# A hybrid attention, S5 and convolution layer on one core: the first head's loads in another order, the S5 branch's tables in another order and further apart, its Toeplitz loads on another queue

## The chip, the core and the metric

The kernel runs on one core of one Trainium2 chip. A core has a matrix engine (TensorE, PE in the profile, with its weight loads as PEld), VectorE (DVE), ScalarE (ACT), GpSimd (POOL), and SyncE (SP), which here only issues transfers. Every engine takes its instructions in the order in which they stand in its queue. The metric is the time of one launch in device microseconds (us); less is better.

## What is computed

One layer of a streaming encoder trunk, for a prompt of 2048 frames of one new stream and for 64 new frames of a running stream with 2048 cached frames. The width is 1024. The normed input is projected; eight attention heads of 64 with a forget gate, an S5 state-space branch and a gated short convolution each make a part of `mix`; an out-projection and a feed-forward layer of 4096 follow.

```python
h = _rms(x, lp['ln1']); proj = h @ lp['w_in']          # q, k, v, forget gate, u, conv inputs
s = q k^T * HEAD_DIM**-0.5 + c_q - c_k                  # c: cumulative log forget gate
p = softmax(where(k_pos <= q_pos, s, NEG_INF)); att = p @ v
h_t = a * h_(t-1) + bbar u_t ;  y = Re(c h) + d u       # S5: 16 groups of 16 channels, 64 complex states
ssm = g * sigmoid(g @ w_glu + b_glu),  g = gelu(y)
conv = gate_b * sum_j w[j] z[t + j],   z = gate_c * hc
x = x + concat[_rms(att), _rms(ssm), _rms(conv)] @ w_out
x = x + relu(_rms(x) @ w_up)**2 @ w_down
```

## The kernel before

The work runs in phases: the in-projection with the first head's row maxima (`phase1`), attention (`attention`), the out-projection, the up- and the down-projection. The change touches only the attention phase, and the loads that stand ahead of it.

**Heads.** A head is 24 units of one or two key tiles of 128 against 512 queries. A unit (`scores`) makes scores `st` in two matmuls (L1239 from `kb` and `q1`, L1240 from `ka` and `q2`), their exponential `p` and its rounded part `ph` on ACT (L1248, L1251), the rest `pl` on DVE (L1252), and, two and three units later, the sums `po` with `v3` (L1260, L1262, L1267). Beside them stand the row maxima of the next head: `mx` on PE (L1149, L1153) and `pm` on DVE (L1154). `load(h)` brings a head's `kb`, `q1` and `ka`; `load_q2` brings one quarter of the queries as `q`, `load_v` the values. `load(h + 1)` is issued at the start of head h. All are issued by SP, in its order. Of the first head, `load(0)` also issues its first `q` and its `v`, and ACT issues a small transfer of its row maxima (`m_d<-mt`, then `q<-m_d`).

**The background.** After each unit `fill(w)` draws steps from a generator, `chain()`: the S5 branch, the attention of the 64 sample frames, and the preparation of the out-projection. A step that yields n is followed only when a clock has moved on by n; the clock moves by 1.68 times the unit's cost, so a bigger yield hands the work out further apart. The scheduler keeps what is drawn in about this order on each engine's queue.

**The S5 branch** (`s5_branch`) loads `u` (`load_u`, `s5ut`), then makes tables for four quarters of its groups (`tables(q)`): on POOL z = u1*bbr and tz = u2*bbi (L859), z + tz (L862) and te = v2*cti (L866); on DVE the part e = v1*ctr (L866) and its sum with te (L870). There is one `te`, one `tz`, and two z, which take turns; PE reads z for the transposes `s5pg` and the products `s5pk` of the quarter (L884, L892). The products go by way of `s5zk` and a store (`kp_d<-s5zk`, L900) to memory, and from there come back as a block Toeplitz matrix `s5mt` (L922, eight loads of 256 KB). The states run as a scan on POOL (L931 to L935) in `s5hs`, of which two pairs of stores (L952, L953) scatter single words to the outputs.

**Completion.** Each transfer of SP or ACT takes one of eight completion semaphores in turn (DMAHW0 to DMAHW7), and waits at its issue until the transfer that last had it is done.

Of the kernel before, what the change touches and what calls it, by code (L numbers as in the profile page):

```python
# [13 lines left out]
ALU = mybir.AluOpType  # L14
# [34 lines left out]
def f32(ap):  # L49
    return ap.bitcast(F32)  # L50
# [735 lines left out]
def s5_branch(g, pool, sp):  # L786

    nc, I, O = g.nc, g.I, g.O
    po, ve, ac = nc.gpsimd, nc.vector, nc.scalar
# [3 lines left out]
    def psum(nm):  # L793
        return g.psum.tile([128, 512], F32, tag="mx", bufs=g.mxb, name=nm)
# [5 lines left out]
    u1, u2, v1, v2, bbr, bbi, ctr, cti = (cut(*d) for _, d in S5P)  # L800
# [45 lines left out]
    e_t = pool.tile([128, G, 17, 16], F32, tag="e", name="s5e")  # L846
# [4 lines left out]
    po.memset(kp[:, :, 0:112], 0.0)  # L851

    def tables(q):
        z = zts[q % 2]
        gs = slice(4 * q, 4 * q + 4)
        sh = [128, 4, 16, 16]
        tz = tt[:, :1024].rearrange("p (g s c) -> p g s c", g=4, s=16)
        for dst, a, b in ((z, u1, bbr), (tz, u2, bbi)):
            g.tc.keep_in_program_order(po.tensor_tensor(  # L859
                dst, a.rearrange("p s g -> p g s")[:, gs].unsqueeze(3).to_broadcast(sh),  # L860
                b[:, gs].unsqueeze(2).to_broadcast(sh), op=ALU.mult))
        po.tensor_tensor(z, z, tz, op=ALU.add)  # L862
        sh = [128, 4, 17, 16]
        te = te_t.rearrange("p (g s c) -> p g s c", g=4, s=17)
        for eng, dst, a, b in ((ve, e_t[:, gs], v1, ctr), (po, te, v2, cti)):
            g.tc.keep_in_program_order(eng.tensor_tensor(  # L866
                dst, a.rearrange("p s g -> p g s")[:, gs].unsqueeze(3).to_broadcast(sh),
                b[:, gs].unsqueeze(2).to_broadcast(sh), op=ALU.mult))
            yield 2
        g.tc.keep_in_program_order(ve.tensor_tensor(e_t[:, gs], e_t[:, gs], te, op=ALU.add))  # L870
        yield 2

    yield from tables(0)
    yield 6
    for q in range(4):
# [3 lines left out]
        z = zts[q % 2]  # L879
        for j in range(2):  # L880
            p = psum(f"s5pg{q}{j}")
# [6 lines left out]
        for j in range(2):  # L888
            p = psum(f"s5pk{q}{j}")
# [16 lines left out]
    for q in range(6):  # L906
        gl = list(range(3 * q, min(3 * q + 3, G)))
        p = psum(f"s5ps{q}")
# [9 lines left out]
        nc.sync.dma_start(hs[hh, 129, :], I[src][0, 0].rearrange("g p -> p g"))  # L918

    mt = pool.tile([128, G, 256], F32, tag="gm", name="s5mt")  # L920
    for t in range(8):
        nc.sync.dma_start(mt[16 * t:16 * t + 16],  # L922
                          g.kp_d[:, :, 16 * (7 - t):16 * (7 - t) + 256].rearrange("g c n -> c g n"))
        yield 1
    r1 = sp.tile([128, 16, G], F32, tag="yg", bufs=3, name="s5r1")
    r2 = sp.tile([128, 16, G], F32, tag="yg", bufs=3, name="s5r2")

# [37 lines left out]
    for half in range(2):  # L965
        ych = pool.tile([128, 3, 8, 128], F32, tag="ych", name=f"s5ych{half}")
        for gq in range(2):
            for a in range(4):
                gg = half * 8 + gq * 4 + a
                p = psum(f"s5py{gg}")  # L970
# [25 lines left out]
        for t in range(8):  # L996
            p = psum(f"s5pg{half}{t}")
# [4 lines left out]
        for t in range(8):  # L1002
            y = gt[:, t, :]
            a = sp.tile([128, NCK], F32, tag="yg", bufs=3, name=f"s5ga{half}{t}")
# [10 lines left out]
    for m in range(2):  # L1015
        st = pool.tile([128, NCK, 8], F32, tag=("hs", "ych")[m], name=f"s5o{m}")
        for t in range(8):
            p = psum(f"s5pz{m}{t}")
# [3 lines left out]
            a = sp.tile([128, NCK], F32, tag="yg", bufs=3, name=f"s5gz{m}{t}")  # L1022
# [145 lines left out]
def attention(ctx, g, fill):  # L1168

    tc, nc = g.tc, g.nc  # L1170
# [7 lines left out]
    ka, kb, q1, v3 = [], [], [], []  # L1178
# [17 lines left out]
    def load(h):  # L1196
        i, hp, e = h % 2, h // 2, h % 2
        r = slice(64 * e, 64 * e + 64)
        qk = g.qk_d[hp]
        nc.sync.dma_start(f32(kb[i])[64:67, :], g.nc_d[:, h, :])  # L1200
        nc.sync.dma_start(f32(kb[i])[0:64, :], qk[0, 1, r, :])
        nc.sync.dma_start(f32(q1[i])[0:64, :], qk[0, 0, r, :])
        nc.sync.dma_start(f32(ka[i])[0:64, :], qk[0, 1, r, :])
        nc.sync.dma_start(f32(ka[i])[64:128, :], qk[1, 1, r, :])
        if h == 0:
            load_q2(0, 3)
            nc.scalar.dma_start(f32(q1[i])[64:67, :], g.m_d)
            load_v(0)

    def load_v(h):  # L1210
        i, hp, e = h % 2, h // 2, h % 2
        nc.sync.dma_start(f32(v3[i])[:, :, 0:128],
                          g.v_d[hp][e])

    def load_q2(h, sb):
        hp, e = h // 2, h % 2
        r = slice(64 * e, 64 * e + 64)
        c = slice(sb * 512, sb * 512 + 512)
        t = pp.tile([128, 512], F32R, tag="q2", bufs=3, name=f"q2{h}_{sb}")
        nc.sync.dma_start(f32(t)[0:64, :], g.qk_d[hp][1, 0, r, c])  # L1220
        nc.sync.dma_start(f32(t)[64:128, :], g.qk_d[hp][0, 0, r, c])
        q2[h, sb] = t
# [4 lines left out]
    po = {}  # L1227
# [69 lines left out]

    units = order()
    total = sum(u[4] for u in units)
    fill(0.1)  # L1300
    load(0)
    pend, pend2 = [], []

    def late(n, m):
# [57 lines left out]
def w_out_tiles(g, pool, tags, dtype, out):  # L1362
    for tag, n in tags:
        t = pool.tile([128, n, D], dtype, tag=tag, name=f"wo_{tag}{len(out)}")
        out += [t[:, j, :] for j in range(n)]


def w_out_load(g, pool, tags):
    k0 = len(g.wo_r)
    w_out_tiles(g, pool, tags, F32, g.wo_r)  # L1370
    for k in range(k0, len(g.wo_r)):
        g.nc.sync.dma_start(g.wo_r[k], g.I["w_out"][0, k * 128:k * 128 + 128, :])
# [482 lines left out]
@with_exitstack  # L1855
def hybrid_step_kernel(ctx, tc, I, O, dbg=None):
    g = setup(ctx, tc, I, O)
    with ExitStack() as c1:
        phase1(c1, g)
    with ExitStack() as c2:  # L1860
        fpool = c2.enter_context(tc.tile_pool(name="fill", bufs=1, side="right", reuse_waits="tile"))
        fsp = c2.enter_context(tc.tile_pool(name="fills", bufs=1, side="right", reuse_waits="tile"))

        def chain():
            for y in s5_branch(g, fpool, fsp):
                if y < 0:
                    yield from sample_attention(g, fpool, fsp, (0, 1))
                    g.idle = True
                    yield from sample_attention(g, fpool, fsp, (2, 3))
                else:  # L1870
                    yield y

            w_out_load(g, fpool, (("hs", 2), ("ych", 2)))
            w_out_tiles(g, fpool, (("u", 4),), F32R, g.wo_h)
            w_out_tiles(g, fpool, (("x1", 2), ("x2", 2)), F32R, g.wo_l)
            yield 4
            for k in range(4, 8):
                w_out_split(g, k)
                yield 0
            yield from out_sample(g, fpool)  # L1880
            while not g.late:
                yield 0
            g.prep[0] = out_prep(g, 0)
            for _ in range(3):
                next(g.prep[0])
                yield 4

        clock = Ctx()
        clock.now, clock.ready, clock.budget = 0.0, 0.0, 0.0
        it = chain()  # L1890

        def side_by_side(*gens):
            ready = {x: clock.now for x in gens}
            while ready:
                x = min(ready, key=ready.get)
                if ready[x] > clock.now:
                    yield ready[x] - clock.now
                y = next(x, None)
                if y is None:
                    del ready[x]  # L1900
                else:
                    ready[x] = clock.now + y
                    if y == 0:
                        yield 0

        g.side_by_side = side_by_side

        def fill(w):

            clock.now += w * 1.68  # L1910
            clock.budget = min(clock.budget + w, 4.0)
            while clock.budget > 0 and clock.now >= clock.ready:
                y = next(it, None)
                if y is None:
                    break
                clock.ready = max(clock.now + y, clock.ready)
                clock.budget -= 0.4 if y > 0 else 1.25

        g.ah = c2.enter_context(tc.tile_pool(name="ah", bufs=1, reuse_waits="tile"))
        g.os = c2.enter_context(tc.tile_pool(name="os", bufs=2, reuse_waits="tile"))  # L1920
        g.ready, g.prep, g.late, g.idle = {}, {}, False, False
        g.fpool, g.fsp = fpool, fsp
        with ExitStack() as c2a:
            attention(c2a, g, fill)
            for _ in it:
                pass
        with ExitStack() as c3:
            phase3a(c3, g)
    g.wts, g.fts, g.first = {}, {}, {}
    with ExitStack() as c6:  # L1930
        g.xp = c6.enter_context(tc.tile_pool(name="both", bufs=1, reuse_waits="tile"))
        with ExitStack() as c4:
            phase_up(c4, g)
        with ExitStack() as c5:
            phase_down(c5, g)
    if dbg is not None:
        dbg(g)
# [30 lines left out]
```

## Time and profile before

| | us |
|---|---|
| median of 3 runs | 2793.95 (2791.91 to 2795.13) |
| the profiled execution | 2794.95 |
| its span, first to last instruction | 2793.2 |
| PE busy in the span | 2699.9 (97%) |
| DVE, ACT, POOL busy | 1681.7, 1230.3, 415.4 |
| mean granted clock of TensorE | 0.979 |
| attention phase | about 543 to 1190 |

Busy time is the time in which an engine works on an instruction. A granted clock of 1.00 is TensorE's full speed, 0.50 its lower level. Idle time of PE, and the part of its busy time that goes to the lower level, are what the phases lose.

### The profile page before, as it was taken

Reading aid. Unit: us, or ns where it says so; the run is one execution under the profiler, and the core shown is the slowest. Engines: PE = TensorE matmul, PEld = TensorE weight load, DVE = VectorE, ACT = ScalarE, POOL = GpSimd, SP = SyncE. Lnnn points to the kernel's source line nnn. Section 1 sums busy time; section 2 is a strip of 40 time slices with the busy share of each in tenths; the row PEclk is TensorE's granted clock in tenths of the full one; section 3 lists DMA queues with packets and bytes.
Section 4 is the critical chain, followed back from the end, with each engine's and each line's share of the span. In section 5 each row is a group of like instructions: output and inputs, shape, how many; then the busy total and the mean of one; then the engine's idle time right before and its main releaser. Section 6 shows DMA issues by size and latency. Waiting matters only on the chain.

```text
span 2793.2 us, 38960 instructions
## 1 busy us (share of the span) xinstructions
PE 2699.9 (97%) x14438; PEld 2341.8 (84%) x14438; DVE 1681.7 (60%) x3375; ACT 1230.3 (44%) x2383; POOL 415.4 (15%) x566
## 2 busy tenths in 40 slices
PE   7999999888899999899989999999999999999999
PEld 7999998755567776688789999999998888888887
DVE  7637468477575576577786686686644344434433
ACT  5424243156577677833265676576641111111110
POOL 2101105123752224432300000000000000000000
PEclk9999999989899999999999999999999999999999
DMA  7636546643644223375545353344354122212123
GB/s 216 186 109 185 165 104 177 111 99 93 108 100 109 72 71 89 116 213 165 177 137 176 131 176 127 133 156 136 128 198 151 51 78 80 78 48 78 49 79 117
DMA packets 358929, 347.13 MB, mean 124 GB/s; under 512 B 43726, under 2 KB 316446, under 8 KB 354734
## 3 DMA queue, kind: packets, MB, share of 16 engines
q1 hardware_dynamic: 356189, 336.87, 41.8%
q0 software_dynamic: 2240, 7.01, 0.8%
q8 instruction: 114, 1.87, 0.3%
q14 instruction: 76, 0.62, 0.1%
q10 hardware_dynamic: 310, 0.75, 0.1%
HBM read 237.05 MB, written 107.46 MB: 123 GB/s over the span
## 4 chain that ended last, share of the span: by engine, by line
PE 85%; DMA 4%; issue 4%; DVE 3%; ACT 2%; POOL 1%; SPq 1%; ACTq 0%; DVEq 0%; POOLq 0%
PE pa L1641 12%; PE pd L107 8%; PE pd L108 8%; PE pd L106 8%; PE pd L1641 6%; PE pb L1641 3%; PE pq L106 3%; PE pq L108 3%; PE pq L107 3%; PE mx L1149 2%; PE po L106 2%; PE st L1239 2%; PE po L107 2%; PE po L108 2%; PE st L1240 2%
## 5 line engine op out<-in xcount | busy, mean ns | idle before, releaser
L1820 DVE TENSOR_TENSOR acc<-acc,pd 128x512 f32<-128x512 f32 x272 | 186.7, 686 | 411.2 <-PE pd L108 406.0
L106 PE MATMUL pd<-dw,fh 128*128 128x512 f32 x1016 | 395.2, 389 | 0.0
L108 PE MATMUL pd<-dw,fl 128*128 128x512 f32 x1016 | 395.2, 389 | 0.0
L107 PE MATMUL pd<-dw,fh 128*128 128x512 f32 x1016 | 395.2, 389 | 0.0
L1789 ACT ACTIVATE fh<-fr 128x512 fp32r<-128x512 f32 x127 | 80.2, 632 | 530.9 <-PE pd L107 520.9
L1252 DVE TENSOR_TENSOR pl<-p,ph 128x512 fp32r<-128x512 f32 (+2 forms) x246 | 171.5, 715 | 110.7 <-ACT ph L1251 104.5
L107 PEld LDWEIGHTS pd<-dw,fh 128*128 128x128 f32 x1016 | 190.7, 188 | 39.7
L108 PEld LDWEIGHTS pd<-dw,fl 128*128 128x128 f32 x1016 | 190.7, 188 | 39.6
L106 PEld LDWEIGHTS pd<-dw,fh 128*128 128x128 f32 x1016 | 190.7, 188 | 39.5
L1154 DVE TENSOR_REDUCE pm<-mx 128x1 f32<-128x512 f32 (+2 forms) x320 | 184.3, 607 | 58.7 <-PE mx L1153 32.3
L1248 ACT ACTIVATE p<-st 128x512 f32<-128x512 f32 (+2 forms) x320 | 164.3, 544 | 89.8 <-PE st L1240 34.2
L1641 PE MATMUL pa<-as,wt 128*128 128x352 f32 x1152 | 201.3, 323 | 0.8 <-ACT sm L1656 0.8
L1641 PEld LDWEIGHTS pa<-as,wt 128*128 128x128 f32 x1152 | 187.3, 188 | 2.0 <-ACT sm L1656 1.3
L106 PE MATMUL pq<-wh,xh 128*128 128x384 f32 (+1 forms) x512 | 179.4, 350 | 5.2 <-ACT xh L233 4.7
L1251 ACT ACTIVATE ph<-p 128x512 fp32r<-128x512 f32 (+2 forms) x320 | 173.8, 581 | 3.9 <-PE po L1262 1.8
L108 PE MATMUL pq<-wh,xl 128*128 128x384 f32 (+1 forms) x512 | 174.5, 341 | 0.5 <-DVE xl L234 0.3
L107 PE MATMUL pq<-wl,xh 128*128 128x384 f32 (+1 forms) x512 | 174.1, 340 | 0.0
L1586 DVE TENSOR_TENSOR wt<-tt,wt 128x512 fp32r<-128x512 f32 x192 | 131.4, 687 | 69.1 <-ACT wt L1585 65.9
L1586 DVE TENSOR_TENSOR w<-wr,w 128x512 fp32r<-128x512 f32 x144 | 99.0, 688 | 87.2 <-ACT w L1585 86.9
L1585 ACT ACTIVATE wt<-tt 128x512 fp32r<-128x512 f32 x192 | 120.4, 627 | 67.2 <-PE pd L1641 66.2
L1240 PE MATMUL st<-q,ka 128*128 128x512 f32 (+2 forms) x320 | 124.4, 393 | 12.0 <-DMA q<-qk_d 12.0
L1149 PE MATMUL mx<-kb,q 66*128 66x512 f32 (+2 forms) x280 | 113.4, 438 | 18.1 <-DVE pm L1154 11.1
(508 smaller groups left out, 6118.6 us busy)
## 6 DMA issues: line engine op xcount, KB each, us to landing
wr<-in_w_up_dram SPq DMA_DIRECT2D x46, 1024.0 KB
f_d<-sm SPq DMA_DIRECT2D x47, 704.0 KB
fr<-f_d SPq DMA_DIRECT2D x128, 256.0 KB
raw<-in_w_in_dram SPq DMA_DIRECT2D x51, 512.0 KB
dr<-in_w_down_dram SPq DMA_DIRECT2D x32, 512.0 KB
qk_d<-stgT SPq DMA_DIRECT2D x16, 768.0 KB
xt<-in_x_prompt_dram SPq DMA_DIRECT2D x16, 512.0 KB
ka<-qk_d SPq DMA_DIRECT2D x16, 512.0 KB
```

The lines of the kernel that those rows point to most:

```text
L106: nc.tensor.matmul(out, lh, rh, start=first, stop=False)
L107: nc.tensor.matmul(out, lh, rl, start=False, stop=False)
L108: nc.tensor.matmul(out, ll, rh, start=False, stop=last)
L1149: nc.tensor.matmul(p[:, :n], q1[0:66, t * 128:t * 128 + 128], kb[0:66, k0 * 128:k0 * 128 + n], start=True, stop=not last)
L1154: nc.vector.tensor_reduce(pm[:, t, c:c + 1], p[:, :n], axis=AX.X, op=ALU.max)
L1240: nc.tensor.matmul(st[:, c0:], ka[i][:, kc], q2[h, sb][:, c0:512], start=False, stop=r < 0)
L1248: nc.scalar.activation(p[:, c0:], st[:, c0:], AF.Exp)
L1251: nc.scalar.activation(ph[:, c0:], p[:, c0:], AF.Copy)
L1252: (nc.gpsimd if g.idle and j else nc.vector).tensor_tensor(pl[:, c0:], p[:, c0:], f32(ph)[:, c0:], op=ALU.subtract)
L1586: ve.tensor_tensor(t[:, 1], x, f32(t)[:, 0], op=ALU.subtract)):
L1641: nc.tensor.matmul(bank, w[:, x, k], a[:, y, k], start=first and k + j == 0, stop=k + j == 5, skip_group_check=not first)
L1820: nc.vector.tensor_tensor(a[:, o], a[:, o], p, op=ALU.add)
```

## The change

There are three parts. First, `load(0)` stands ahead of `fill(0.1)`, so that SP issues the first head's loads before `s5ut`, and the two 64-row loads of `ka` are one of 128 rows, for every head. Second, `tables` takes te first, then z beside the part on DVE, then tz beside the sum on DVE, then z + tz, with yields of 2, 3, 3 and 2 (in sum 10, before 6). Third, the eight loads of `s5mt` become a generator, `toeplitz`, which yields 4 ahead of each, issues them on ACT's queue, and runs beside the sample attention of the second pair of head pairs.

```diff
--- before.py
+++ after.py
@@ -851,23 +851,29 @@
     po.memset(kp[:, :, 0:112], 0.0)
 
     def tables(q):
+        gs = slice(4 * q, 4 * q + 4)
         z = zts[q % 2]
-        gs = slice(4 * q, 4 * q + 4)
-        sh = [128, 4, 16, 16]
         tz = tt[:, :1024].rearrange("p (g s c) -> p g s c", g=4, s=16)
-        for dst, a, b in ((z, u1, bbr), (tz, u2, bbi)):
-            g.tc.keep_in_program_order(po.tensor_tensor(
-                dst, a.rearrange("p s g -> p g s")[:, gs].unsqueeze(3).to_broadcast(sh),
-                b[:, gs].unsqueeze(2).to_broadcast(sh), op=ALU.mult))
-        po.tensor_tensor(z, z, tz, op=ALU.add)
-        sh = [128, 4, 17, 16]
         te = te_t.rearrange("p (g s c) -> p g s c", g=4, s=17)
-        for eng, dst, a, b in ((ve, e_t[:, gs], v1, ctr), (po, te, v2, cti)):
+
+        def outer(eng, dst, a, b):
+            sh = [128, 4, dst.shape[2], 16]
             g.tc.keep_in_program_order(eng.tensor_tensor(
                 dst, a.rearrange("p s g -> p g s")[:, gs].unsqueeze(3).to_broadcast(sh),
                 b[:, gs].unsqueeze(2).to_broadcast(sh), op=ALU.mult))
-            yield 2
-        g.tc.keep_in_program_order(ve.tensor_tensor(e_t[:, gs], e_t[:, gs], te, op=ALU.add))
+
+        def add(eng, dst, x):
+            g.tc.keep_in_program_order(eng.tensor_tensor(dst, dst, x, op=ALU.add))
+
+        outer(po, te, v2, cti)
+        yield 2
+        outer(po, z, u1, bbr)
+        outer(ve, e_t[:, gs], v1, ctr)
+        yield 3
+        outer(po, tz, u2, bbi)
+        add(ve, e_t[:, gs], te)
+        yield 3
+        add(po, z, tz)
         yield 2
 
     yield from tables(0)
@@ -918,10 +924,14 @@
         nc.sync.dma_start(hs[hh, 129, :], I[src][0, 0].rearrange("g p -> p g"))
 
     mt = pool.tile([128, G, 256], F32, tag="gm", name="s5mt")
-    for t in range(8):
-        nc.sync.dma_start(mt[16 * t:16 * t + 16],
-                          g.kp_d[:, :, 16 * (7 - t):16 * (7 - t) + 256].rearrange("g c n -> c g n"))
-        yield 1
+
+    def toeplitz():
+        for t in range(8):
+            yield 4
+            ac.dma_start(mt[16 * t:16 * t + 16],
+                         g.kp_d[:, :, 16 * (7 - t):16 * (7 - t) + 256].rearrange("g c n -> c g n"))
+
+    g.toeplitz = toeplitz
     r1 = sp.tile([128, 16, G], F32, tag="yg", bufs=3, name="s5r1")
     r2 = sp.tile([128, 16, G], F32, tag="yg", bufs=3, name="s5r2")
 
@@ -1200,8 +1210,7 @@
         nc.sync.dma_start(f32(kb[i])[64:67, :], g.nc_d[:, h, :])
         nc.sync.dma_start(f32(kb[i])[0:64, :], qk[0, 1, r, :])
         nc.sync.dma_start(f32(q1[i])[0:64, :], qk[0, 0, r, :])
-        nc.sync.dma_start(f32(ka[i])[0:64, :], qk[0, 1, r, :])
-        nc.sync.dma_start(f32(ka[i])[64:128, :], qk[1, 1, r, :])
+        nc.sync.dma_start(f32(ka[i]), qk[:, 1, r, :])
         if h == 0:
             load_q2(0, 3)
             nc.scalar.dma_start(f32(q1[i])[64:67, :], g.m_d)
@@ -1297,8 +1306,8 @@
 
     units = order()
     total = sum(u[4] for u in units)
+    load(0)
     fill(0.1)
-    load(0)
     pend, pend2 = [], []
 
     def late(n, m):
@@ -1866,7 +1875,7 @@
                 if y < 0:
                     yield from sample_attention(g, fpool, fsp, (0, 1))
                     g.idle = True
-                    yield from sample_attention(g, fpool, fsp, (2, 3))
+                    yield from side_by_side(sample_attention(g, fpool, fsp, (2, 3)), g.toeplitz())
                 else:
                     yield y
 
```

SP's queue at the start of attention (rows with the semaphores that they wait for; `kb_6570` and `v_6573` are the first head's, `kb_6577` the second's), before:

```order
L1200 DMA kb_6570<-nc_d 3x2048 [waits DMAHW1_49,DMAHW2_49,DMAHW0_49,DMAHW4_49,DMASW7_49,DVE_49]
L1201 DMA kb_6570<-qk_d_60 64x2048
L808 DMA s5ut_6586<-u_d 88x2048 [waits DMAHW7_49]
L1202 DMA q_6571<-qk_d_60 64x2048 [waits DMAHW3_49,PE_49]
L1203 DMA ka_6572<-qk_d_60 64x2048
L1204 DMA ka_6572<-qk_d_60 64x2048 [waits DMAHW5_49]
L1220 DMA q_3_6593<-qk_d_60 64x512 [waits DMAHW6_49,PE_49]
L1221 DMA q_3_6593<-qk_d_60 64x512 [waits DMAHW7_49]
L1212 DMA v_6573<-v_d_64 128x16x128 [waits DMAHW0_49]
L1200 DMA kb_6577<-nc_d 3x2048 [waits DMAHW1_49,PE_49]
L1201 DMA kb_6577<-qk_d_60 64x2048 [waits DMAHW2_49]
```

and in the changed kernel:

```order
L1210 DMA kb_6570<-nc_d 3x2048 [waits DMAHW1_49,DMAHW2_49,DMAHW0_49,DMAHW4_49,DMASW7_49,DVE_49]
L1211 DMA kb_6570<-qk_d_60 64x2048
L1212 DMA q_6571<-qk_d_60 64x2048 [waits PE_49]
L1213 DMA ka_6572<-qk_d_60 128x1x2048 [waits DMAHW3_49]
L1229 DMA q_3_6585<-qk_d_60 64x512 [waits PE_49]
L1230 DMA q_3_6585<-qk_d_60 64x512 [waits DMAHW5_49]
L1221 DMA v_6573<-v_d_64 128x16x128 [waits DMAHW6_49]
L808 DMA s5ut_6595<-u_d 88x2048 [waits DMAHW7_49]
L1210 DMA kb_6577<-nc_d 3x2048 [waits DMAHW0_49,PE_49]
L1211 DMA kb_6577<-qk_d_60 64x2048 [waits DMAHW1_49]
L1212 DMA q_6578<-qk_d_60 64x2048 [waits DMAHW2_49]
```

The `q_3` loads no longer wait for DMAHW6 and DMAHW7 as set by ACT's two small transfers; `v` and `s5ut` do. `s5ut` stands behind `v`, and in front of the second head's loads.

POOL's queue at the tables (`s5zt` and `s5zk` are the two z, and `s5zt` the tz too), before:

```order
L859 TENSOR_TENSOR s5zt<-s5sc 128x1024 x2
L961 TENSOR_SCALAR s5bg<-s5bg 128x2
L862 TENSOR_TENSOR s5zt<-s5zt 128x1024
L866 TENSOR_TENSOR s5te<-s5sc 128x1088
L859 TENSOR_TENSOR s5zk<-s5sc 128x1024
L859 TENSOR_TENSOR s5zt<-s5sc 128x1024
L862 TENSOR_TENSOR s5zk<-s5zk,s5zt 128x1024
L866 TENSOR_TENSOR s5te<-s5sc 128x1088
L859 TENSOR_TENSOR s5zt<-s5sc 128x1024 x2
L862 TENSOR_TENSOR s5zt<-s5zt 128x1024
```

and in the changed kernel:

```order
L861 TENSOR_TENSOR s5te<-s5sc 128x1088
L861 TENSOR_TENSOR s5zt<-s5sc 128x1024 x2
L971 TENSOR_SCALAR s5bg<-s5bg 128x2
L866 TENSOR_TENSOR s5zt<-s5zt 128x1024
L861 TENSOR_TENSOR s5te<-s5sc 128x1088
L861 TENSOR_TENSOR s5zk<-s5sc 128x1024
L861 TENSOR_TENSOR s5zt<-s5sc 128x1024
L866 TENSOR_TENSOR s5zk<-s5zk,s5zt 128x1024
L861 TENSOR_TENSOR s5te<-s5sc 128x1088
L861 TENSOR_TENSOR s5zt<-s5sc 128x1024 x2
```

`s5te` stands ahead of the products of its quarter, in each.

The Toeplitz loads in SP's queue before (head 2; `kb_6577` is the fourth head's):

```order
L922 DMA s5mt<-kp_d 16x16x256
L922 DMA s5mt<-kp_d 16x16x256 [waits DMAHW1_49]
L1164 DMA q_6571<-mt_8117 1x16x128 [waits DMAHW2_49,DVE_49]
L922 DMA s5mt<-kp_d 16x16x256 x2
L922 DMA s5mt<-kp_d 16x16x256 [waits DMAHW5_49]
L922 DMA s5mt<-kp_d 16x16x256 [waits DMAHW6_49]
L1200 DMA kb_6577<-nc_d 3x2048 [waits DMAHW7_49,PE_49]
L1201 DMA kb_6577<-qk_d_61 64x2048 [waits DMAHW0_49]
L1202 DMA q_6578<-qk_d_61 64x2048 [waits DMAHW1_49]
L1203 DMA ka_6575<-qk_d_61 64x2048 [waits DMAHW2_49,PE_49]
L1204 DMA ka_6575<-qk_d_61 64x2048 [waits DMAHW3_49]
L922 DMA s5mt<-kp_d 16x16x256 [waits DMAHW4_49]
```

SP's queue at the same load in the changed kernel:

```order
L906 DMA kp_d<-s5zk 16x2x368
L1174 DMA q_6571<-mt_8048 1x16x128
L906 DMA kp_d<-s5zk 16x2x368
L1210 DMA kb_6577<-nc_d 3x2048
L906 DMA kp_d<-s5zk 16x2x368
L1211 DMA kb_6577<-qk_d_61 64x2048
L1212 DMA q_6578<-qk_d_61 64x2048
L1213 DMA ka_6575<-qk_d_61 128x1x2048
L1281 DMA mix_d<-ot_1_8254 64x512
L1282 DMA l_d<-ot_1_8254 1x512
L924 DMA s5hs<-in_state_ssm_re_dram 64x16x1
L924 DMA s5hs<-in_state_ssm_im_dram 64x16x1
```

and the first of the Toeplitz loads in ACT's queue of the changed kernel, in head 2:

```order
L931 DMA s5mt<-kp_d 16x16x256 [waits DMAHW5_49]
L1061 ACTIVATE sa_i<-sa_pi 4x128 [waits PE_49]
L1280 ACTIVATE ot_2_8465<-po_2_7859 65x512 [waits DMAHW3_49,DMAHW2_49]
L1260 ACTIVATE ph_3_5_8481<-p_3_5_8480 128x512 [waits Activation_49]
L1257 ACTIVATE p_0_0_8518<-st_0_0_8514 128x512 [waits DVE_49,PE_49]
L1257 ACTIVATE p_3_6_8538<-st_3_6_8535 128x512 [waits DVE_49,PE_49]
L1260 ACTIVATE ph_0_0_8519<-p_0_0_8518 128x512 [waits Activation_49]
L1257 ACTIVATE p_3_7_8545<-st_3_7_8542 128x512 [waits DVE_49,PE_49]
```

On SP two of the stores `kp_d` now stand around the first row of `load(3)`, and none of the Toeplitz loads; the states' loads `s5hs`, from which the scan starts, stand behind it. On ACT the eight stand some 18 rows apart, from head 2 into head 3.

## Rows read from the trace of the kernel before

**Rows 1.** Windows of 20 us: busy us of each engine (instructions), granted TensorE clock, DMA share, GB/s.

```profile
540.00:560.00 20.00, 7.23 (x31) 5.26 (x31) 4.91 (x18) 4.09 (x7) 4.07 (x7) 0.63 0.79 105
560.00:580.00 20.00, 19.17 (x81) 12.35 (x80) 12.69 (x23) 10.97 (x24) 0.00 (x0) 0.77 1.01 239
580.00:600.00 20.00, 19.99 (x123) 14.96 (x122) 14.29 (x25) 16.18 (x41) 1.79 (x2) 1.00 0.40 93
600.00:620.00 20.00, 12.53 (x45) 7.17 (x44) 16.49 (x16) 5.91 (x11) 18.87 (x9) 0.75 0.00 0
620.00:640.00 20.00, 19.88 (x92) 13.46 (x90) 16.12 (x31) 12.85 (x28) 5.00 (x2) 0.82 0.07 18
640.00:660.00 20.00, 16.33 (x69) 9.26 (x67) 11.41 (x19) 13.34 (x28) 6.99 (x3) 0.83 0.71 167
660.00:680.00 20.00, 16.77 (x78) 11.36 (x76) 17.74 (x25) 8.31 (x19) 9.62 (x5) 0.83 0.16 39
...
720.00:740.00 20.00, 13.32 (x63) 8.82 (x61) 8.27 (x10) 8.43 (x17) 18.83 (x24) 0.91 1.07 140
740.00:760.00 20.00, 18.89 (x65) 11.12 (x65) 11.19 (x20) 11.36 (x24) 17.81 (x39) 0.67 0.65 144
```

**Rows 2.** Timeline of SP's queue: start, us, line, out<-in.

```profile
539.73 0.44 SPq L1220 DMA_DIRECT2D q<-qk_d  x1
...
542.32 0.60 SPq L1212 DMA_DIRECT2D v<-v_d  x1
543.02 10.52 SPq L1200 DMA_DIRECT2D kb<-nc_d  x1
```

**Rows 3.** Timeline of PE, with idle time before and its releaser.

```profile
555.07 1.62 PE L1240 MATMUL st<-q,ka 128*128 128x512 f32 x3 [11.61 <-DMA q<-qk_d]
...
559.81 0.67 PE L1260 MATMUL po<-ph,v 128*65 128x512 f32 x1
...
567.92 0.28 PE L1149 MATMUL mx<-kb,q 66*128 66x256 f32 x1
```

**Rows 4.** Timeline of POOL.

```profile
540.08 0.71 POOL L419 DMA_DIRECT2D out_dram<-z  x1 [6.65 <-DVE zs L401]
...
606.51 2.12 POOL L866 TENSOR_TENSOR s5te<-s5sc 128x1088 f32<-128x1088 f32 x1
...
635.00 6.32 POOL L859 TENSOR_TENSOR s5zt<-s5sc 128x1024 f32<-128x1024 f32 x2 [16.05 <-PE s5pk L892]
...
644.92 2.14 POOL L866 TENSOR_TENSOR s5te<-s5sc 128x1088 f32<-128x1088 f32 x1
```

**Rows 5.** Timeline of DVE.

```profile
608.67 3.09 DVE L870 TENSOR_TENSOR s5e<-s5e,s5te 128x1088 f32<-128x1088 f32 x1 [3.51 <-POOL s5te L866]
...
612.02 2.17 DVE L1252 TENSOR_TENSOR pl<-p,ph 128x512 fp32r<-128x512 f32 x1
...
647.10 1.29 DVE L870 TENSOR_TENSOR s5e<-s5e,s5te 128x1088 f32<-128x1088 f32 x1 [4.40 <-POOL s5te L866]
...
648.31 3.22 DVE L1252 TENSOR_TENSOR pl<-p,ph 128x512 fp32r<-128x512 f32 x5
```

**Rows 6.** Timeline of SP's queue at load(3).

```profile
719.43 0.27 SPq L1200 DMA_DIRECT2D kb<-nc_d  x1
```

**Rows 7.** Tile s5mt: duration of one issue in ns, min, median, max.

```profile
L922 SPq DMA_DIRECT2D s5mt<-kp_d x8: 303/452/1870, 707.2 to 723.8; - x8
```

**Rows 8.** Chain that ended last, 714 to 745: start us, us, what.

```profile
718.89 8.69 DMA s5mt<-kp_d
...
727.60 19.29 DMA q<-qk_d
```

**Rows 9.** Timeline of PE after the Toeplitz loads.

```profile
738.83 0.55 PE L1149 MATMUL mx<-kb,q 66*128 66x256 f32 x1 [6.26 <-issue]
```

**Rows 10.** Tile s5hs, 720 to 800: its scattered stores, first and last start.

```profile
L952 POOL DMA_DIRECT2D out_dram<-s5hs x2: 849/874/899, 723.3 to 779.4; - x2
...
DMA to landing us min/median/max: 8.9/15.6/15.8
```

## The prediction

> **What bounds the kernel now.** I read the busy times first: TensorE is busy for 97% of the span (the table above), so time can come only from where it stands still, or runs at its lower clock. Next come the windows of the attention phase, which the change touches [rows 1]. The window from 580 to 600 is what an undisturbed stretch looks like: 19.99 of 20 us busy at a granted clock of 1.00. Each other window loses its idle time, and of its busy time the share by which the clock is under 1.00 (work at 0.50 takes twice as long). From 540 to 580 that is 12.77 + 7.23 x 0.37 + 0.83 + 19.17 x 0.23 = 20.7 us; from 600 to 640, 7.47 + 12.53 x 0.25 + 0.12 + 19.88 x 0.18 = 14.3; from 640 to 660, 3.67 + 16.33 x 0.17 = 6.4; from 660 to 680, 3.23 + 16.77 x 0.17 = 6.1; from 720 to 760, 6.68 + 13.32 x 0.09 + 1.11 + 18.89 x 0.33 = 15.2. The idle time always comes first, and the lower clock behind it. So a wait that goes gives back about its double.
>
> The timelines then say which wait each dip is. At 540 SP's issue of the first head's `q` stands until 539.73, `v` until 542.32, and the next small load takes 10.52 us to issue [rows 2]; TensorE waits 11.61 us for that `q`, until 555.07, then starts on `v` at 559.81 and on the next head's maxima at 567.92 [rows 3]. At 600 and 640 DVE stands before its sum, 3.51 and 4.40 us, for `s5te`, which POOL makes last of a table [rows 4, 5]. From 720 on TensorE stands 6.26 us before a maximum of the next head [rows 9]; the chain goes through a Toeplitz load (8.69 us) and a `q` load of 19.29 us behind it [rows 8].
>
> **The change part by part.** All is costed against the profiled execution, 2794.95 us, which is 1.0 above the median.
>
> First head. The changed queue issues `q` and its other half without the wait for ACT's small transfers. So the wait of 11.61 us for `q` goes, but `v` now waits for the first of these, which is done at about 539.7 (where the old `q` was let go [rows 2]). It is thus issued 2.6 us earlier than at 542.32. POOL's scattered store of 540.08 [rows 4] comes in just behind it, and transfers then crawl, as the 10.52 us of one issue show [rows 2], until about 553.5. I take it that most of `v` lands behind that, near 555, where before it was 559.81. The scores ahead of it are done by then: 4.8 us are gained at `v`. But `s5ut` (704 KB, by its 88 x 2048 words) now stands between `v` and the second head's loads, where at 239 GB/s [rows 1] it takes 3.0 us, so the maxima at 567.92 hardly come earlier. What is late next is `q1` of the second head. I keep 2 us of the 4.8; bounds: -2 (`q1` comes 3.0 us later, less some slack) and 8 (`v` is through before the stall).
>
> Tables, order. In the changed queue `te` is the first product of its quarter, so the sum on DVE no longer waits for two products and an addition. From 600 to 640 DVE lost, over an undisturbed run of the same operations, the wait of 3.51, 3.09 - 1.29 = 1.8 at the sum, 2.17 - 0.64 = 1.5 at a `pl` (0.64 is a fifth of the 3.22 us for five) and about twice that, 3, at the two behind it [rows 5]: 9.8 us. The wait and the slow sum go, 5.3 of 9.8; the slow `pl` stay, since POOL still does four operations a table. That share of 14.3 us is 7.7, and I take 8; bounds 3.5 (the wait alone) and 14.3. From 640 to 660 the `te` stood behind products that themselves waited 16.05 us until TensorE's `s5pk` had read the z that they overwrite [rows 4]. Now `te` goes ahead of these, and the 4.40 us go, while the `pl` beside it were fast [rows 5]. I take 4.5, bounds 2 (another wait of half its size takes its place) and 6.4. At 660 to 680 nothing of the order changes: 0, bounds -4 (a wait like that at 647 comes in) and 3 (half of its 6.1 goes).
>
> Tables, spacing. Ten instead of six due times each puts some 16 more ahead of all that follows, 8 of which the Toeplitz loads give back. The background's work comes later by about a quarter of a head, and the order of the queues shows it caught up by the out-projection's preparation, which still stands in the last head. So it costs nothing at the end; without that cover it would cost up to that quarter, 647 / 8 / 4 = 20 us by the phase's length in the table.
>
> Toeplitz loads. Eight issues leave SP, with a median of 452 ns [rows 7], so `load(3)`, which began at 719.43 [rows 6], is issued some 3.6 us earlier, and 1.75 MB, seven of the eight loads, no longer stand ahead of it in the transfer engines. What gives TensorE its 6.26 us [rows 9] then lands in time. Of 15.2 I take 10: two stores `kp_d` stand around the first row of `load(3)` now, and each waits for ACT and DVE to finish `s5zk`. Bounds 5 and 15.
>
> [...]
>
> ACT gets eight issues of about 0.45 us, 3.6 us in all, at places where it is busy 11.36 of 20 us [rows 1], so most is hidden by its idle time. With the `kp_d` stores closer together (a store must land before the next copy into the one buffer) I take a cost of 3, bounds 0 and 6.
>
> Sum: 2 + 8 + 4.5 + 0 + 10 - 3 = 21.5 us; 2794.95 - 21.5 = 2773.5, or about 2772.5 by the median's measure. **I predict 2773.** With the terms' bounds added as squares the spread is about 10 down and 11 up: 2762 to 2783.
>
> **The rivals.**
>
> *The scattered stores hit another load.* The scan's two pairs of stores began at 723.3 and 779.4 and took up to 15.8 us to land [rows 10]; that of 723.3 lies in front of the 6.26 us [rows 9]. In the changed SP queue the scan's inputs come behind `load(3)`, so it starts some 5 to 10 us after that load instead of before it, and the second pair falls near `load(4)`. If that load is issued less than about 16 us before the stores land, TensorE waits there as it did here, for 8 to 15 us: 2773 + 8 to 15 = 2781 to 2788. Against it: without the 1.75 MB ahead of it the load may be through first.
>
> *The engines' clash stays.* The slow `pl` (2.17 against 0.64 us) and the slow sum come from POOL working beside DVE, not from the order. If that sets the dips at 600 to 660, both table terms vanish: 2794.95 - 2 - 10 + 3 = 2786, 2783 to 2791. For it: POOL does the same operations. Against: they are now spread over more units, and the waits are real.
>
> [...]
>
> *ACT is blocked by its own loads.* Each Toeplitz load on ACT waits for the one before it, with the next exponentials and `ph` behind it in the queue, for which TensorE waits. They stand 18 instructions apart; ACT did 24 in 20 us [rows 1], so 15 us apart. A load of 8.69 us costs nothing, one of 19.29 [rows 8] costs 4.3. It ends slower than before by over 0.2% (5.6 us) where seven waits cost 21.5 + 5.6, 3.9 us each, from a landing of 18.9 us on: 2801 and more. Against it: only a transfer next to scattered stores took that long.
>
> **How the numbers follow.** Forecast 0.55, second stall 0.20, clash 0.16, ACT blocked 0.09. 0.2% of the time, 5.6 us, is about what a measurement of this kernel can tell from no change: under 2788.4 is faster, over 2799.5 slower. Faster: 0.55 + 0.16 + 0.09 = 0.80, with 0.04 of the second and 0.07 of the third case in the same; same: 0.04 + 0.07 + 0.01 = 0.12; slower 0.08. The range for 8 in 10 goes from 2758 (the first head's and the first table's term at their upper bounds, and no cost on ACT: 2773 - 6 - 6.3 - 3) to 2790, which leaves out the slow case, and some of the clash and of the forecast's lower tail.
>
> **What would show it.** In the changed profile: TensorE has no wait for `q` near 543, but one for `v` that ends near 555; DVE's sum with `te` shows no wait for POOL in all four; `pl` of about 2 us are still there; no SP row of `s5mt`, and no idle of over 3 us at the fourth head's first maximum; ACT's rows behind `s5mt` wait for nothing. Wrong would be: a new wait for `load(4)` 10 to 16 us behind the second pair of `s5hs` stores; a clock under 0.85 from 590 to 660 with the waits gone; idle time of TensorE on `p` or `ph` behind an `s5mt` issue; or sample attention that runs past the last head.

## The result, and the profile after

The changed kernel took 2910.06 us (median of four runs, 2907.45 to 2913.21) against 2792.93 for the kernel before in the same job: ratio 1.0419, 95% interval 1.0401 to 1.0437. It is 117 us slower, where 21 us faster was forecast, and far outside the range of 2758 to 2790. Its profiled execution has a span of 2909.5 us at a mean granted clock of 0.962.

On the page of the profile, TensorE's busy time grew by 11.8 us and its idle time by 104.5 (from 93.3 to 197.8 of the span). Transfers make 9% of the chain that ended last instead of 4, and the score matmul that reads `ka` waits 64.6 us for loads of `q`, instead of 12.0. In the changed kernel:

```profile
PE 2711.7 (93%) x14438; PEld 2346.2 (81%) x14438; DVE 1692.4 (58%) x3377; ACT 1231.3 (42%) x2383; POOL 408.3 (14%) x564
...
PE 78%; DMA 9%; DVE 6%; ACT 3%; issue 2%; SPq 2%; POOL 1%; ACTq 0%; DVEq 0%; POOLq 0%
...
L1249 PE MATMUL st<-q,ka 128*128 128x512 f32 (+2 forms) x320 | 126.1, 396 | 64.6 <-DMA q<-qk_d 64.6
```

and in the kernel before:

```profile
PE 85%; DMA 4%; issue 4%; DVE 3%; ACT 2%; POOL 1%; SPq 1%; ACTq 0%; DVEq 0%; POOLq 0%
...
L1240 PE MATMUL st<-q,ka 128*128 128x512 f32 (+2 forms) x320 | 124.4, 393 | 12.0 <-DMA q<-qk_d 12.0
```

The windows that answer to [rows 1], with one of 10 us in between (busy us of each engine and its instructions, granted clock, DMA share, GB/s):

```profile
540.00:560.00 20.00, 2.33 (x13) 1.63 (x11) 2.36 (x11) 0.00 (x0) 2.78 (x6) 0.67 0.27 68
560.00:580.00 20.00, 16.13 (x52) 10.10 (x53) 6.04 (x9) 9.34 (x17) 0.00 (x0) 0.67 0.79 166
580.00:600.00 20.00, 3.22 (x15) 2.26 (x13) 2.47 (x5) 1.07 (x3) 0.00 (x0) 0.50 0.37 93
590.00:600.00 10.00, 0.00 (x0) 0.00 (x0) 0.00 (x0) 0.00 (x0) 0.00 (x0) 0.50 0.13 52
600.00:620.00 20.00, 18.82 (x92) 13.39 (x93) 11.71 (x21) 14.19 (x33) 0.00 (x0) 0.80 0.44 109
620.00:640.00 20.00, 16.80 (x87) 10.36 (x85) 18.86 (x24) 9.71 (x24) 12.02 (x7) 0.97 0.17 34
640.00:660.00 20.00, 18.11 (x70) 11.79 (x71) 19.02 (x27) 10.50 (x21) 8.37 (x4) 0.69 0.05 15
660.00:680.00 20.00, 16.44 (x82) 9.53 (x80) 18.69 (x22) 14.01 (x28) 11.17 (x4) 1.00 0.63 134
720.00:740.00 20.00, 19.88 (x104) 13.50 (x105) 18.54 (x37) 15.09 (x28) 0.12 (x1) 1.00 0.32 81
740.00:760.00 20.00, 20.00 (x132) 16.06 (x130) 7.37 (x19) 14.91 (x30) 0.00 (x0) 1.00 0.44 98
```

From 720 to 760 there is no dip, but the work of that stretch comes some 25 to 50 us later now (`load(3)` starts at 743.96 instead of 719.43), so it isn't the same work. The first head is far worse, and in the 10 us from 590 to 600 TensorE does nothing at all, while the DMA engines are busy for a share of 0.13, which is as much as 2 of the 16, and move 52 GB/s. Before, while the second head's loads ran (560 to 580), the share was 1.01, at 239 GB/s [rows 1]. The timeline of TensorE, which answers to [rows 3], has two waits there, and six more of over 10 us behind them:

```profile
560.37 1.62 PE L1249 MATMUL st<-q,ka 128*128 128x512 f32 x3 [17.00 <-DMA q<-qk_d]
...
601.17 0.76 PE L1249 MATMUL st<-q,ka 128*128 128x512 f32 x1 [17.95 <-DMA q<-qk_d]
...
691.21 0.58 PE L1159 MATMUL mx<-kb,q 66*128 66x256 f32 x1 [12.34 <-ACT s5zk L900]
...
781.51 0.69 PE L1269 MATMUL po<-ph,v 128*65 128x512 f32 x1 [15.25 <-ACT ph L1260]
...
890.41 0.77 PE L1249 MATMUL st<-q,ka 128*128 128x512 f32 x1 [17.41 <-DMA q<-qk_d]
...
988.24 0.80 PE L1249 MATMUL st<-q,ka 128*128 128x512 f32 x1 [12.27 <-DMA q<-qk_d]
...
1088.04 0.80 PE L1159 MATMUL mx<-kb,q 66*128 66x512 f32 x1 [11.97 <-ACT s5gt L1010]
...
1183.94 0.79 PE L1248 MATMUL st<-q,kb 67*128 67x512 f32 x1 [12.33 <-ACT p L1257]
```

SP's queue (start, us, line) shows what was being loaded ahead of the second: the second head's `ka`, and 20 us later a load that takes 21.64 us to issue.

```profile
561.47 0.56 SPq L1213 DMA_DIRECT2D ka<-qk_d  x1
...
582.23 21.64 SPq L808 DMA_DIRECT2D s5ut<-u_d  x1
```

This repeats in every head: each of the eight loads of `ka` is followed, 27 to 40 us behind its issue, by one of the eight waits. They are 116.5 us in sum, and the kernel before has a single wait of over 10 us in attention (11.61 [rows 3]). Four of the eight are for `q`, which stands behind `ka` in the same queue. In the other four TensorE waits for ACT, and ACT had itself waited for a transfer (us in total, times, longest):

```profile
ACT ot L1280 <- DMA mix_d<-ot: 20.9, 1, 20.9
...
ACT wo_e L1388 <- DMA wo_u<-in_w_out_dram: 14.7, 1, 14.7
ACT s5zk L900 <- DMA kp_d<-s5zk: 14.0, 2, 12.9
...
ACT ot L1280 <- DMA l_d<-ot: 13.2, 1, 13.2
```

So it isn't `q` alone that comes late, but whatever SP's queue has next behind `ka`.

What the forecast said of the tables came true in the small: DVE's sums with `te`, which waited 3.51 and 4.40 us [rows 5], wait for nothing (no bracket), and the first is still slow beside POOL:

```profile
635.98 2.60 DVE L866 TENSOR_TENSOR s5e<-s5e,s5te 128x1088 f32<-128x1088 f32 x1
...
695.44 1.28 DVE L866 TENSOR_TENSOR s5e<-s5e,s5te 128x1088 f32<-128x1088 f32 x1
```

### The profile page after: what moved, and what is told of

The parts are those of the page before. It is cut to its first block, busy times and chain, and to the rows that moved or that the text cites. A ratio compares the mean times of both kernels' runs of the same rounds, so it can differ in the third digit from the quotient of the medians.

```text
span 2909.5 us, 38932 instructions
## 1 busy us (share of the span) xinstructions
PE 2711.7 (93%) x14438; PEld 2346.2 (81%) x14438; DVE 1692.4 (58%) x3377; ACT 1231.3 (42%) x2383; POOL 408.3 (14%) x564
## 4 chain that ended last, share of the span: by engine, by line
PE 78%; DMA 9%; DVE 6%; ACT 3%; issue 2%; SPq 2%; POOL 1%; ACTq 0%; DVEq 0%; POOLq 0%
PE pa L1650 12%; PE pd L107 8%; PE pd L108 8%; PE pd L106 8%; PE pd L1650 6%; DMA q<-qk_d 3%; PE pb L1650 3%; PE pq L108 2%; PE pq L106 2%; PE pq L107 2%; PE mx L1159 2%; PE po L106 2%; PE po L107 2%; PE po L108 2%; PE st L1249 1%
## 5 line engine op out<-in xcount | busy, mean ns | idle before, releaser
L1261 DVE TENSOR_TENSOR pl<-p,ph 128x512 fp32r<-128x512 f32 (+2 forms) x248 | 178.0, 736 | 154.6 <-ACT ph L1260 149.9
L1249 PE MATMUL st<-q,ka 128*128 128x512 f32 (+2 forms) x320 | 126.1, 396 | 64.6 <-DMA q<-qk_d 64.6
```

Source lines behind the costliest of these rows:

```text
L1249: nc.tensor.matmul(st[:, c0:], ka[i][:, kc], q2[h, sb][:, c0:512], start=False, stop=r < 0)
L1261: (nc.gpsimd if g.idle and j else nc.vector).tensor_tensor(pl[:, c0:], p[:, c0:], f32(ph)[:, c0:], op=ALU.subtract)
```

## The experiments

**Which part costs it.** Four kernels undo one part each, all four with `ka` in two transfers:

```diff
-        nc.sync.dma_start(f32(ka[i]), qk[:, 1, r, :])
+        nc.sync.dma_start(f32(ka[i])[0:64, :], qk[0, 1, r, :])
+        nc.sync.dma_start(f32(ka[i])[64:128, :], qk[1, 1, r, :])
```

> The changed kernel with ka loaded in two transfers of 64 rows again, all else as changed. Theory 1 (the merged ka load, whose outermost dimension is 2, runs on two of the 16 DMA engines; every load behind it waits there): the whole loss goes, and what the other parts give is left: 2777 us, 2768 to 2790. Theory 2 (the first head's order), theory 3 (Toeplitz loads on ACT's queue) and theory 4 (background later by the tables' spacing) each expect 2880 or more, since their part is still there.

2796.91 us, ratio 0.9999 (0.9990 to 1.0007). The whole loss lies in the merged load. But what the other parts should have given, 21 us, isn't there either.

`e4_old_tables` puts the old `tables` back on top of that.

> As e1_split, and the tables in their old order and spacing. Theory 1: slower than e1_split by the forecast's two table terms, 8 to 12.5 us, so about 2788; no change against e1_split would say that the order of the tables gives nothing. Theory 4 alone expects the loss to go here and not in e1_split.

2798.45 us, 1.0007 (0.9997 to 1.0018): in this company the new tables give some 2 us, within the intervals, not 8 or more.

`e5_old_mt` puts the Toeplitz loads back on SP.

> As e1_split, and the Toeplitz loads on SP as before. Theory 1: slower than e1_split by the forecast's term for them less ACT's cost, about 7 to 10 us, so about 2786. Theory 3 alone expects the loss to go here and not in e1_split.

2786.90 us, 0.9960 (0.9948 to 0.9972): 11 us by the ratios faster than `e1_split`, not slower. In this company the move to ACT costs.

`e6_old_first` swaps `load(0)` and `fill(0.1)` back.

> As e1_split, and the first draw of the background ahead of load(0) as before, so s5ut is issued early again. Theory 1: the first head's term is 2 us at most, and with two ka loads the second half of q waits for ACT's small transfer again, so within 3 us of e1_split. Theory 2 alone expects the loss to go here and not in e1_split.

2792.28 us, 0.9985 (0.9976 to 0.9995): the new order of the first head costs some 4 us, though the two intervals still touch. The windows after the start, of `e1_split`:

```profile
560.00:580.00 20.00, 17.02 (x62) 10.88 (x60) 8.30 (x15) 4.50 (x9) 0.00 (x0) 0.67 1.01 200
580.00:600.00 20.00, 19.31 (x96) 13.96 (x96) 11.07 (x20) 15.54 (x36) 0.00 (x0) 0.81 0.61 150
```

and of `e6_old_first`:

```profile
560.00:580.00 20.00, 19.07 (x78) 12.13 (x78) 12.34 (x21) 10.49 (x23) 0.00 (x0) 0.76 1.02 240
580.00:600.00 20.00, 19.99 (x116) 14.64 (x116) 13.31 (x24) 15.71 (x37) 0.00 (x0) 0.94 0.39 99
```

By the forecast's own formula these are 2.98 + 17.02 x 0.33 + 0.69 + 19.31 x 0.19 = 13.0 us lost against 0.93 + 19.07 x 0.24 + 0.01 + 19.99 x 0.06 = 6.7. The stretch behind the first wait loses it, where `s5ut` now runs ahead of the second head's loads.

**Why the merged load costs.** First the merge alone, in the kernel before, and then a cut into two transfers by columns, so that both still have an outermost dimension of 2 in memory:

```diff
-        nc.sync.dma_start(f32(ka[i]), qk[:, 1, r, :])
+        nc.sync.dma_start(f32(ka[i])[:, 0:1024], qk[:, 1, r, 0:1024])
+        nc.sync.dma_start(f32(ka[i])[:, 1024:2048], qk[:, 1, r, 1024:2048])
```

> The kernel before with only its two ka loads merged into one. Theory 1 (the merged load runs on two of the 16 DMA engines): 110 to 140 us slower than before, 2905 to 2935. The rival (the merge costs only together with the other parts, say with s5ut ahead of the second head's loads) expects it within 20 us of before.

2909.21 us, 1.0410 (1.0395 to 1.0425).

> The changed kernel with ka in two transfers again, but cut by columns: each brings 128 rows of half the columns, so each still has an outermost dimension of 2. Theory 1: as slow as the changed kernel, 2895 to 2935. The rival (what costs is that there is one transfer instead of two, by the turn of the semaphores or by its size) expects the time of e1_split, about 2797.

2919.43 us, 1.0444 (1.0429 to 1.0459). The number of transfers isn't it. Both have the distant halves in one transfer, though, so the last pair has none that joins them: each half of 64 rows is cut in two, at row 62 or at row 48.

```diff
-        nc.sync.dma_start(f32(ka[i])[0:64, :], qk[0, 1, r, :])
-        nc.sync.dma_start(f32(ka[i])[64:128, :], qk[1, 1, r, :])
+        for a in (0, 1):
+            for o, n in ((0, 62), (62, 2)):
+                nc.sync.dma_start(f32(ka[i])[64 * a + o:64 * a + o + n, :], qk[a, 1, r, :][o:o + n, :])
```

> The kernel before with each 64-row load of ka cut into 62 and 2 rows. [...] If what costs in the merged load is its joining of two halves that lie far apart in memory, or that it is one transfer of 1 MB: within 15 us of before.

2894.76 us, 1.0352 (1.0335 to 1.0370).

> The control of e13_rows62: each 64-row load of ka cut into 48 and 16 rows, as many transfers of as many bytes. [...] If four transfers instead of two are what costs in e13: as slow as e13.

2808.32 us, 1.0045 (1.0028 to 1.0061). As many transfers of as many bytes differ by 86 us by where they are cut. What `ka`'s matmuls waited for with 62 and 2 rows (the last two numbers), and a window of it, with a DMA share of 0.61 at 133 GB/s, in which TensorE still stands:

```profile
L1241 PE MATMUL st<-q,ka 128*128 128x512 f32 (+2 forms) x320 | 125.3, 396 | 58.5 <-DMA q<-qk_d 58.5
```

```profile
590.00:600.00 10.00, 0.00 (x0) 0.00 (x0) 0.00 (x0) 0.00 (x0) 0.00 (x0) 0.50 0.61 133
```

and with 48 and 16:

```profile
L1241 PE MATMUL st<-q,ka 128*128 128x512 f32 (+2 forms) x320 | 125.2, 395 | 17.0 <-DMA q<-qk_d 17.0
```

```profile
590.00:600.00 10.00, 9.99 (x62) 7.04 (x61) 9.56 (x16) 9.13 (x23) 3.55 (x3) 1.00 0.35 64
```

Four transfers instead of two, cut at row 48, cost 13 us (1.0045).

**Where the forecast gain went.** In `e1_split` the one long wait of TensorE between 796 and 820 is before a maximum of the next head (us in total, times, longest):

```profile
PE mx L1159 <- DMA q<-qk_d: 12.7, 1, 12.7
```

SP issued `load(4)` at

```profile
796.92 0.37 SPq L1210 DMA_DIRECT2D kb<-nc_d  x1
```

and POOL the second pair of the scattered `s5hs` stores at 798.4, between that load and its use:

```profile
L962 POOL DMA_DIRECT2D out_dram<-s5hs x2: 849/874/899, 741.6 to 798.4; - x2
...
DMA to landing us min/median/max: 9.9/11.8/21.3
```

So `e8_split_rows` keeps everything of `e1_split`, and writes the states as rows of 64 words, from a transpose:

```diff
-        po.dma_start(O[o][0, 0].rearrange("g p -> p g"), hs[lo, j, :])
-        po.dma_start(O[o + 1][0, 0].rearrange("g p -> p g"), hs[hi, j, :])
+        p = psum(f"s5st{j}")
+        nc.tensor.transpose(p[:16, :128], hs[:, j, :], g.ident)
...
+        nc.sync.dma_start(O[o][0, 0], sv[:, 0:64])
+        nc.sync.dma_start(O[o + 1][0, 0], sv[:, 64:128])
```

> As e1_split, and the four stores of the S5 states, which scatter single words, are made from a transpose on TensorE, as rows of 64 words. If what e1_split loses near 800 us (12.7 us of TensorE before a maximum of the next head) is load(4) held up by the second pair of these stores, and part of the dip at 740 by the first: 14 to 20 us under e1_split, about 2780. If it is the Toeplitz loads themselves, side by side with load(4) or on ACT's queue: as e1_split, 2797.

2781.34 us, 0.9954 (0.9940 to 0.9967): 12.6 us by the ratios. The window of `e1_split`:

```profile
800.00:820.00 20.00, 6.62 (x26) 3.56 (x24) 4.23 (x6) 5.43 (x11) 18.55 (x27) 0.73 0.97 125
```

and of `e8_split_rows`, where `load(4)` is issued at 797.75, no earlier:

```profile
800.00:820.00 20.00, 16.48 (x70) 9.68 (x68) 10.34 (x16) 11.94 (x25) 18.69 (x24) 0.91 1.01 217
```

At nearly the same DMA share 217 GB/s are moved instead of 125, and TensorE is busy for 16.48 us instead of 6.62. The edit changes only the stores, but two things of them: they are rows instead of single words, and SP issues them instead of POOL. Which of the two helps wasn't tried by itself. The first pair of stores shows no such gain. From 740 to 760 `e1_split` loses 4.04 + 15.96 x 0.09 = 5.5 us and `e8_split_rows` 2.77 + 17.23 x 0.17 = 5.7:

```profile
740.00:760.00 20.00, 15.96 (x70) 10.24 (x69) 12.29 (x20) 10.72 (x24) 18.83 (x25) 0.91 0.39 67
740.00:760.00 20.00, 17.23 (x65) 10.39 (x65) 14.53 (x21) 11.93 (x27) 18.65 (x23) 0.83 0.27 67
```

**Order or spacing of the tables.** `e7_tables_only` is the kernel before with the new `tables` alone.

> The kernel before with only the new tables. If the parts add up, e1_split less what e5 and e6 gave against it: 2797 - 10 - 5 = 2782, ratio about 0.995. If the tables alone also move the scan's stores onto a load, as in e1_split: 2790 or more. If the clash of POOL and DVE decides: as before.

2782.18 us, 0.9955 (0.9942 to 0.9969), as the sum of the parts said. But they add up on this path alone: with the old tables the first head's order and the loads on ACT cost 2 us together (`e4`), with the new ones 4 + 11. Its window from 720 to 760, with the Toeplitz loads still on SP:

```profile
720.00:760.00 40.00, 36.63 (x162) 21.88 (x160) 32.34 (x50) 22.89 (x47) 36.06 (x56) 0.94 0.85 122
```

It loses 3.37 + 36.63 x 0.06 = 5.6 us, where the two windows of before lost 15.2 [rows 1]. Much of that only comes later. From 780 to 840 the kernel before loses 0.4 us, and `e7` 2.78 + 57.22 x 0.06 = 6.2:

```profile
780.00:840.00 60.00, 59.65 (x327) 41.66 (x326) 40.52 (x71) 45.53 (x95) 28.49 (x35) 1.00 0.46 113
780.00:840.00 60.00, 57.22 (x287) 37.81 (x286) 41.21 (x66) 39.87 (x84) 35.63 (x57) 0.94 0.54 117
```

Then its two halves: the new order with yields of 2, 2 and 2 (`e11`), and the old order with yields of 4, 4 and 2 (`e12`).

> The kernel before with the tables in their new order, but due times of 6 in sum as before. If DVE's waits for POOL were the cost (the forecast's table terms), it has most of what e7 has, 8 to 12 us under before, ratio 0.9957 to 0.997. If the clash of POOL and DVE close together is the cost, within 4 us of before.

2795.68 us, 1.0005 (0.9995 to 1.0015): nothing.

> The kernel before with the tables in their old order, handed out with due times of 10 in sum as in the change. If the waits were the cost, within 4 us of before; if the clash of operations close together, most of what e7 has, 8 to 12 us under before, ratio 0.9957 to 0.997.

2792.21 us, 0.9985 (0.9975 to 0.9995): 4 us, the edge of what the one theory expected and half of the other. The window of the tables, in the kernel before:

```profile
600.00:680.00 80.00, 65.51 (x279) 41.26 (x277) 61.75 (x89) 40.42 (x82) 40.48 (x18) 0.81 0.24 56
```

in the new order alone:

```profile
600.00:680.00 80.00, 69.88 (x286) 44.61 (x284) 69.36 (x92) 41.22 (x84) 36.93 (x17) 0.81 0.26 64
```

in the new spacing alone:

```profile
600.00:680.00 80.00, 69.93 (x324) 42.94 (x323) 74.08 (x105) 47.64 (x95) 38.82 (x17) 0.94 0.31 77
```

and with both:

```profile
600.00:680.00 80.00, 70.59 (x320) 43.81 (x319) 76.91 (x105) 48.69 (x97) 38.76 (x17) 0.89 0.26 62
```

Idle and slow time are 14.5 + 12.4 = 26.9 us before, 10.1 + 13.3 = 23.4 with the order, 10.1 + 4.2 = 14.3 with the spacing, and 9.4 + 7.8 = 17.2 with both. In this stretch the spacing does most of it. It takes away both suspects, though: in `e12` too no sum on DVE waits for `te`. What speaks against the waits is `e11`, where none waits either, but the third sum takes 3.48 us instead of 1.29 [rows 5], and a `pl` 0.89 us on average from 590 to 700, its three shapes together, instead of 0.74:

```profile
639.46 3.48 DVE L866 TENSOR_TENSOR s5e<-s5e,s5te 128x1088 f32<-128x1088 f32 x1
```

`e12` gives most of what it cleared back later, at one place:

```profile
762.87 1.62 PE L1240 MATMUL st<-q,ka 128*128 128x512 f32 x3 [20.54 <-DMA q<-qk_d]
```

There SP issued `q` at 747.59 only, behind Toeplitz loads and a store of `ot` for which it had waited 18.0 us (us in total, times, longest):

```profile
SPq L1272 <- ACT ot L1271: 18.0, 1, 18.0
```

That the order spares `e7` this wait, by shifting the queues against each other, is argued from the two traces and wasn't tried by itself.

**Versions that beat both kernels.** The new tables and the states as rows, with all else as before (`e9`), and the same with the Toeplitz loads on ACT (`e10`):

> The kernel before with the new tables (e7) and the S5 states stored as rows (e8). If the scattered stores are what is lost behind 740 and 800 in e7 (5.4 + 4.3 and 2.9 + 3.3 us of idle and slow time), 5 to 10 us under e7: about 2775, ratio 0.991 to 0.994. If those dips have another cause, as e7, 0.9955.

2778.02 us, 0.9936 (0.9918 to 0.9954): 5 us under `e7` by the ratios, with intervals that overlap.

> As e8 (new tables, Toeplitz loads on ACT, states as rows), with the first head's order of before. If the first head's order costs what e6 showed, 4 to 5 us under e8, about 2777. Against e9 it differs only in the Toeplitz loads: if these cost only by what the stores then hit, the two are equal within 3 us; if issuing on ACT costs by itself, e9 is 7 us or more faster.

2778.67 us, 0.9938 (0.9926 to 0.9950). Without scattered stores of the states the queue that issues the Toeplitz loads makes no difference that these intervals, some 5 us to either side, can show.

## Why the prediction was wrong

**The step that failed** is the one that isn't in its sum. The merged load stands in the description of the change, and no sentence of the prediction prices it: its term was put at nothing without a reason. The only load of the first head that has a duration is `s5ut`, at 239 GB/s. The cost is 115 to 117 us: `e1_split` takes it away, `e2_merge_only` makes it alone, and `e13_rows62` against `e14_rows48`, 2894.76 against 2808.32 us, shows that the rows at which it is cut decide here, not how many transfers there are or how far apart the halves lie. Cut into 48 and 16 rows the load costs 13 us, with 2 or 62 rows outermost 99 to 125. (A cut at row 62 might cost by where it lies, but `e2` and `e3` have no such cut.) That the merged load runs on two of the DMA engines is the author's reading of the share of 0.13 in the window from 590 to 600; in `e3`, from 580 to 590, the share was 0.14 at 50 GB/s. By an estimate from its 52 GB/s, a megabyte takes 20 us even when nothing else runs, in each of eight heads. That what is queued behind it waits for its part on these two engines fits the eight waits, but the profile doesn't show single DMA engines. The kernels whose load has 2 rows outermost were slow (the changed kernel at 1.0419 of before, `e2` at 1.0410, `e3` at 1.0444), and so was that with 62 and 2 (`e13`, 1.0352); that with 64 (`e1`, 0.9999) and, but for the 13 us, that with 48 and 16 (`e14`, 1.0045) were not. By what rule the counts decide, and on how many engines any of these ran, no run shows. The changed queue had shown the merge, as `128x1x2048` where two rows of `64x2048` had stood.

With `ka` in two transfers (`e1`) the forecast's own terms came to nothing instead of 21 us, and each of them failed or was right by luck:

**First head: +2 forecast, -4 measured** (`e6` against `e1`; by the author's reading of the queue, which no row shows, the second half of `q` waits for ACT's transfer again with two loads of `ka`, so it isn't quite the term that was forecast). The waits for ACT's transfers moved as forecast: before, the issue of `q` (L1220) waited 16.1 us for `m_d<-mt`; in the changed kernel that of `v` (L1221) waits 10.7 us for it, and that of `s5ut` (L808) 5.5 us for `q<-m_d`. The mechanism was named, `s5ut` ahead of the second head's loads, and sized too small. `v` is first used 2.0 us earlier than before (557.83 against 559.81 [rows 3]), not 4.8, and the stretch behind it loses more than that.

**Tables: 12.5 forecast, 12.5 measured (`e7`), which is luck.** The step "DVE's waits for `te` go, and give their share of the dips" failed: they went, and `e11` gained nothing. The spacing, which was costed at 0, took 12.6 us from the stretch of the tables (`e12`), and order and spacing together gave the 12.5. The rival of the clash fits `e11`, but it was wrong that the change wouldn't touch the time. Why spacing helps is open: the `pl` stay slow (from 590 to 700 0.89 us on average in `e12` and 0.82 in `e7`, 0.74 before, three shapes together), and DVE is busier from 600 to 680, 74.08 us against 61.75.

**Toeplitz loads: +10 - 3 forecast, -11 measured** (`e5` against `e1`), and 0 without the scattered stores (`e10` against `e9`). The reading behind the +10 doesn't hold: the `q` load of 19.29 us, which stands behind a Toeplitz load in the chain [rows 8], ran from 727.60 to 746.89, and the wait of 6.26 us had ended at 738.83 [rows 9]. So that load isn't what TensorE waited for there, and the profile names no releaser. With the new tables the dip shrank to 5.6 us while the loads were still on SP (`e7`), though a good part came back behind it. That the dip hung on the scan's stores is not shown either: from 740 to 760 `e8` loses as much as `e1`. Its cause stays open.

**The rival of the scattered stores** was right to the place: in `e1_split` the second pair lands on `load(4)` and costs 12.7 us of waiting, within its 8 to 15. With it, what the tables had gained was used up. It was given a chance of 0.20, though its own working (the pair falls near `load(4)`) spoke for more. Its time of 2781 to 2788 was still too low for `e1`, 2796.91, as it kept the other terms.

**ACT blocked by its own loads** didn't happen: in `e1_split` no row of ACT waits for one, and none of the eight issues took more than 0.34 us.

## What to carry to other kernels

Before two transfers are made one, look at the outermost count: here a load whose count was 2 in memory moved 52 GB/s, at a share of 0.13 of the DMA engines, and TensorE waited 12 to 18 us behind each. A wait that ends last in a dip need not be its cause: take the wait away alone, and space the work alone, before crediting either. When work moves, ask what else is in flight where it lands; here four stores of 4 KB each, as single words from POOL or as rows from SP, decided whether 12.6 us came or went (`e8` against `e1`).

## What was not expected of the hardware

The kernel's time hung on the rows at which a load was cut: 62 + 2 rows against 48 + 16 made 86 us of difference for the same bytes. At a share of 0.13 the merged load moved 52 GB/s (by an estimate 26 for each engine, if it ran on two), and an issue on SP behind it lasted 21.64 us. Four kilobytes of single words, stored by POOL, took up to 21.3 us to land; 125 GB/s were moved beside them, and 217 where the same words went out from SP as rows.
